# A hybrid encoder trunk: the gate's low-rank path formed from its own mixed input, and the first head group's gating placed in the stream beside the second group's recurrence

## The chip, the cores and the metric

The kernel runs on one core of one Trainium2 chip. A core has five instruction streams that run side by side: PE (TensorE, matrix multiplication), DVE (VectorE), ACT (ScalarE), POOL (GpSimd) and SP (SyncE, which only issues transfers here). Each stream executes in its own order. PE has a second row in the profile, PEld, for its weight loads. The metric is the device time of one execution in microseconds (us); lower is better. The time before is the median of three runs.

## What is computed

Two residual layers over 512 tokens of width 1024, each a token mixer and a gated convolution feed-forward part. The change touches the second layer's mixer alone, an RWKV-7 time mixing with 16 heads of 64:

```python
xx = token_shift(h) - h
xr = h + xx * mu[0]                     # likewise xw, xk, xv, xa, xg
r = xr @ w_r;  k = xk @ w_k;  v = xv @ w_v
w = -softplus(-(w0 + tanh(xw @ w1) @ w2)) - 0.5     # low rank, 64
a = sigmoid(a0 + (xa @ a1) @ a2)                    # low rank, 64
g = sigmoid(xg @ g1) @ g2                           # low rank, 160
...
y = wkv7_scan(r_h, decay, k_h, v_h, -kk, kk * a_h)  # 512 steps in time
...
return (y * g) @ w_o
```

`h` is the RMS-normed residual stream. The gate `g` is needed only when the recurrence has its result `y`.

## The kernel before

Activations lie transposed: 8 tiles of 128 channels by 512 tokens. Every matrix product with weights is done in three matmuls per tile (`mm3`, L284 to L286): high part by high part, high by low, low by high, each 128x128 by 128x512. `split` (L212 on ACT, L213 on DVE or POOL) makes the parts. `weights` loads 128x1024 of a weight matrix into a ring of two tiles `w` (called `w32` in the code) and splits it into a ring of four tiles `wh` and `wl`.

The layer runs in these stages:

- The feed-forward part of layer 0 (`ffn`). Beside it `make_parts` splits the matrices `wk` and `wv` ahead and stores the parts in memory, so that later loads need no split.
- `rwkv_first`: the low-rank first factors for w and a (`l1`), then those for g (`g1a`, `g1b`), then `r`. The low-rank products are taken from the operand `hx` that is not yet divided by the norm and not yet shifted, once with weights scaled by `1 - mu` and once by `mu`; `shifted` then multiplies both results by the norm `rb` and adds the second one shifted by a token. For w and a that is 2 products of 24 matmuls. For g it is 48 matmuls for 128 of the 160 columns and 24 for the other 32 twice. The three tiles of `sigmoid(xg @ g1)`, called `sg`, are stored to memory (`sgd`). After that each tile of `h` is normalized in place, `mix` forms `xr` from it (one ACT operation, one DVE operation, then the split), and `r` takes 12 matmuls for each of the 8 tiles of its first half (`wra`) and as many for the second half (`wrb`).
- `pairs`, for the 8 pairs of heads, woven with `projections` (`k` and `v`).
- `scan(0)`, then `scan(1)`: the recurrence in chunks of 64 tokens, 8 chunks for each group of 4 pairs of heads; I number the 16 chunks c0 to c15. A chunk is a chain: PE L1066, DVE copy L1068 (`wt`), PE L1079, copies L1080 on DVE and L1081 on ACT (`vu`), PE L1086, DVE L1089, and then L1066 of the next chunk. `load` brings each chunk's operands by SP. `invert(1)` is woven into scan(0); it prepares matrices that scan(1) needs. `finish` normalizes the result of two chunks, and after every second call it gates it (L1133, L1135, L1138, L1139), with weights that `gate_weights` has loaded and split at chunk 1 of each scan.
- `project` multiplies by `w_o`: 12 matmuls for each of 8 output tiles and each group, 192 in all. Group 0's half may start when group 0 is gated. It adds to `h`, which `back` reloads from memory (`hd`) since the tile in the chip holds the normalized `h`.

`weave` sets the order around the change. It takes steps of a main generator (the scan), and after each step it takes steps of a `fill` generator (the rest of `projections` in scan(0), `project` in scan(1)), `rate` of them on average. A scheduler then fixes each engine's order from that, from the free tiles of each ring and from the marks that `issue_after` sets. In the profile's lines the rings' names are `w`, `wh`, `wl`; `mxh` and `mxl` are the parts of an activation tile.

Of the kernel before, what the change touches and what calls it, by code (L numbers as in the profile page):

```python
# [19 lines left out]
P = 128  # L20
# [10 lines left out]
RATES = ((1.9, 2), (1.9, 6, 2.2), (0.8, 2, 2), (0.7, 2), (2, 2), (0.7, 6, 2.2))  # L31
LEAD = 6
# [43 lines left out]
def layout(inp):  # L76
# [34 lines left out]
    a["g1a"] = g1[:, :, :P].reshape(P, 1024)  # L111
    a["g1b"] = np.concatenate([g1[:, :, P:], g1[:, :, P:]], axis=2).reshape(P, 512)
# [31 lines left out]
class Emit:  # L144
    def __init__(self, ctx, tc, A, out):
# [24 lines left out]
        self.wd = {n: [dp.tile([P, 2, 1024], F32, name=f"{n}d{m}") for m in range(KT)] for n in PARTS}  # L170
        self.n = self.turn = 0
# [69 lines left out]
    def make_parts(self, pool):  # L241

        nc = self.nc
        at = [(n, m, slice(c, c + 512)) for n in PARTS for m in range(KT) for c in (0, 512)]
        w = []
        for i in range(len(at) + 1):
            with self.tc.issue_after(self.last(mybir.EngineType.Activation)):
                if i < len(at):
                    n, m, c = at[i]
                    w.append(pool.tile([P, 512], F32, tag="pw", bufs=2, name=self.uid("pw")))  # L250
                    nc.sync.dma_start(w[i], self.A[n][m][:, c])
                if i:
                    n, m, c = at[i - 1]
                    for j, x in enumerate(self.split(pool, w[i - 1], [P, 512], "pw", bufs=1)):
                        nc.sync.dma_start(self.wd[n][m][:, j, c], x.bitcast(F32))
            yield

    def parts(self, n, m, whole):
# [13 lines left out]
        return 512, t  # L272

# [310 lines left out]
    def rwkv(self, gain):  # L584
        nc, tc, A = self.nc, self.tc, self.A
        V, S, G = nc.vector, nc.scalar, nc.gpsimd
        with ExitStack() as ctx:
# [7 lines left out]
            r.sgd = dp.tile([3, P, T], F32, name="sgd")  # L595
# [12 lines left out]
            def mix(i, k):  # L608
# [5 lines left out]
                return self.operand(t, lo_eng=(G, V)[k % 2])  # L614
# [6 lines left out]
    def rwkv_first(self, r, ep):  # L621
# [5 lines left out]
        r.sg = [ep.tile([P, T], F32R, name=f"sg{i}") for i in range(3)]  # L627

# [3 lines left out]
        def lowrank(n, w):  # L632
            a = self.acc()
            self.dense(a[0:n], w, hx, ncol=n)
            return a[0:n]
# [9 lines left out]
        def shifted(now, before, n):  # L645
            t, u = tmp("lt", 2), tmp("lu", 2, T + 1)
            G.memset(u[:, 0:1], 0.0)
            V.tensor_tensor(t[0:n], now, rb[0:n], ALU.mult)
            V.tensor_tensor(u[0:n, 1:], before, rb[0:n], ALU.mult)
            G.tensor_tensor(t[0:n], t[0:n], u[0:n, 0:T], ALU.add)  # L650
            return t
# [3 lines left out]
        t = shifted(*lw, P)  # L655
        S.activation(t[0:64], t[0:64], AF.Tanh)

        for j, x in enumerate(r.lr):
            hi, lo = slice(64 * j, 64 * j + 64), slice(64 - 64 * j, 128 - 64 * j)
            S.copy(x[hi], t[hi])  # L660
            V.tensor_tensor(x[lo], t[hi], x[hi].bitcast(F32), ALU.subtract)
# [4 lines left out]
        for kk in range(4):  # L666
            w = self.weights(A["wra"][kk])
            for j in range(2):
# [4 lines left out]
                for m in range(4):  # L673
                    self.mm3(accs[m], self.wcols(w, j * 512 + m * P, P), xs[k], k == 0, k == KT - 1)
        for m in range(4):
            S.copy(r.rt[0][:, m, :], accs[m])


        for i, (x, n) in enumerate(((ga, P), ((gb[0:32], gb[32:64]), 32))):
            t = shifted(*x, n)[0:n]  # L680
            S.activation(t, t, AF.Tanh, scale=0.5)
            V.tensor_scalar(t, t, 0.5, 0.5, ALU.mult, ALU.add)
            if i == 0:
                S.copy(r.sg[0], t)
                V.tensor_tensor(r.sg[1], t, r.sg[0].bitcast(F32), ALU.subtract)
            else:
                self.stack(r.sg[2], t)
        for i, n in enumerate((P, P, 96)):
            nc.sync.dma_start(r.sgd[i, 0:n], r.sg[i][0:n].bitcast(F32))
# [13 lines left out]
    def rwkv_main(self, r, ctx, gain):  # L703
# [38 lines left out]
        def projections():  # L742

            load = Ahead([lambda n=n, m=m: self.parts(n, m, m % 3 == 2) for n in PARTS for m in range(KT)])
# [258 lines left out]

        def gate_weights(g):
            if not sg:
                for i, n in enumerate((P, P, 96)):
                    sg.append(ep.tile([P, T], F32R, name=f"sg{i}"))
                    nc.sync.dma_start(sg[i][0:n].bitcast(F32), r.sgd[i, 0:n])
# [9 lines left out]
        chunks, outs, gated = {}, {}, set()  # L1018

        def load(g, c):  # L1020
            ps = slice(4 * g, 4 * g + 4)
# [12 lines left out]
        left, sg = [], []  # L1034
# [67 lines left out]
        def finish(g, b, y):  # L1102
# [18 lines left out]
            if b % 2 == 1:  # L1121
                hs = slice((b - 1) * P, (b + 1) * P)
                yield
                if b == 1:
# [158 lines left out]
```

## Time and profile before

| what | us |
|---|---|
| median of three runs | 1319.26 (1318.08 to 1319.82) |
| the profiled execution, its own time | 1317.32 |
| its span, first to last instruction | 1315.5 |
| mean granted TensorE clock | 0.978 of full speed |
| PE busy | 1272.7 |
| DVE busy | 848.5 |
| ACT busy | 623.8 |

A line of a timeline gives the start and the length in us, the engine, the line of the kernel, the operation, the tile written and the tiles read, their shapes and how often, and in brackets how long the engine sat idle before it and what it waited for. An engine's name with a q (ACTq, SPq) marks the issue of a transfer. A line of the stretch view gives the stretch, its length, and then for PE, PEld, DVE, ACT and POOL the busy us in it with the number of instructions started, then the granted clock, the share of the DMA engines and GB/s. PE's matmuls are pipelined: a line says 0.39 us for one of 128x512, while the next one starts 0.23 us after it.

### The profile page before, as it was taken

Reading aid. Unit: us, or ns where it says so; the run is one execution under the profiler, and the core shown is the slowest. Engines: PE = TensorE matmul, PEld = TensorE weight load, DVE = VectorE, ACT = ScalarE, POOL = GpSimd, SP = SyncE. Lnnn points to the kernel's source line nnn. Section 1 sums busy time; section 2 is a strip of 40 time slices with the busy share of each in tenths; the row PEclk is TensorE's granted clock in tenths of the full one; section 3 lists DMA queues with packets and bytes.
Section 4 is the critical chain, followed back from the end, with each engine's and each line's share of the span. In section 5 each row is a group of like instructions: output and inputs, shape, how many; then the busy total and the mean of one; then the engine's idle time right before and its main releaser. Section 6 shows DMA issues by size and latency. Waiting matters only on the chain.

```text
span 1315.5 us, 19526 instructions
## 1 busy us (share of the span) xinstructions
PE 1272.7 (97%) x7618; PEld 1031.3 (78%) x7618; DVE 848.5 (64%) x1365; ACT 623.8 (47%) x1062; POOL 142.8 (11%) x152
## 2 busy tenths in 40 slices
PE   8999999999999999999999998898999999999996
PEld 6878888888888888787777766676888888888886
DVE  5565488788874444865869785656687777772223
ACT  5444455555554333565657644333554444442221
POOL 3100200000000010310111012332300000000001
PEclk9999999999999999999979996999999999999998
DMA  7332345555556753245877786881333232333322
GB/s 259 88 113 80 106 151 170 167 168 174 166 173 211 224 150 108 79 136 157 251 220 205 225 209 147 207 221 41 96 96 97 96 96 96 97 92 91 101 89 76
DMA packets 100461, 188.55 MB, mean 143 GB/s; under 512 B 16912, under 2 KB 47760, under 8 KB 100368
## 3 DMA queue, kind: packets, MB, share of 16 engines
q10 hardware_dynamic: 36448, 109.46, 27.2%
q1 hardware_dynamic: 63920, 77.84, 20.7%
q8 instruction: 60, 0.98, 0.3%
q14 instruction: 33, 0.27, 0.1%
HBM read 146.70 MB, written 40.57 MB: 142 GB/s over the span
## 4 chain that ended last, share of the span: by engine, by line
PE 78%; DVE 9%; ACT 3%; issue 2%; DMA 2%; POOL 1%; ACTq 0%; DVEq 0%; SPq 0%; POOLq 0%
PE mm L284 8%; PE mm L285 8%; PE mm L286 8%; PE e L284 5%; PE e L286 5%; PE e L285 5%; PE us L284 5%; PE us L286 5%; PE us L285 5%; PE aux L284 5%; PE aux L286 5%; PE aux L285 5%; DVE tt L971 1%; DVE pr L970 1%; PE us L1066 1%
## 5 line engine op out<-in xcount | busy, mean ns | idle before, releaser
L212 ACT CAST wh<-w 128x512 fp32r<-128x512 f32 (+1 forms) x361 | 220.1, 612 | 398.8 <-PE mm L285 97.1
L213 DVE TENSOR_TENSOR wl<-w,wh 128x512 fp32r<-128x512 f32 x353 | 243.8, 692 | 186.9 <-ACT wh L212 182.8
L284 PE MATMUL mm<-mxh,wh 128*128 128x512 f32 x392 | 161.2, 412 | 0.6 <-DVE h L1166 0.4
L285 PE MATMUL mm<-mxl,wh 128*128 128x512 f32 x392 | 155.7, 397 | 0.6 <-DVE mxl L1139 0.6
L286 PE MATMUL mm<-mxh,wl 128*128 128x512 f32 x392 | 155.9, 398 | 0.3 <-DVE wl L213 0.3
L311 POOL TENSOR_TENSOR ss<-ss,sq 128x512 f32<-128x512 f32 x30 | 40.7, 1357 | 777.3 <-issue 594.8
L284 PEld LDWEIGHTS mm<-mxh,wh 128*128 128x128 f32 x392 | 74.8, 191 | 20.1 <-issue 3.2
L507 ACT ACTIVATE cv<-z,par 128x512 f32<-128x512 f32 x88 | 71.7, 817 | 36.0 <-DVE z L505 35.9
L286 PEld LDWEIGHTS mm<-mxh,wl 128*128 128x128 f32 x392 | 74.7, 191 | 17.3 <-DVE wl L213 0.6
L285 PEld LDWEIGHTS mm<-mxl,wh 128*128 128x128 f32 x392 | 74.8, 191 | 16.3 <-DVE mxl L1139 1.3
L284 PE MATMUL e<-mxh,wh 128*128 128x512 f32 x216 | 84.5, 391 | 0.0
L284 PE MATMUL us<-mxh,wh 128*128 128x512 f32 (+1 forms) x216 | 84.4, 391 | 0.0
L286 PE MATMUL us<-mxh,wl 128*128 128x512 f32 (+1 forms) x216 | 84.1, 389 | 0.0
L285 PE MATMUL us<-mxl,wh 128*128 128x512 f32 (+1 forms) x216 | 84.1, 389 | 0.0
L285 PE MATMUL e<-mxl,wh 128*128 128x512 f32 x216 | 84.0, 389 | 0.0
L286 PE MATMUL e<-mxh,wl 128*128 128x512 f32 x216 | 84.0, 389 | 0.0
L508 DVE SCALAR_TENSOR_TENSOR cv<-z,par,cv 128x512 f32<-128x512 f32 x88 | 66.1, 752 | 23.9 <-ACT cv L507 23.9
L284 PE MATMUL aux<-mxh,wh 128*128 128x512 f32 x208 | 81.2, 391 | 0.2 <-ACT wh L212 0.2
L286 PE MATMUL aux<-mxh,wl 128*128 128x512 f32 x208 | 81.1, 390 | 0.0
L285 PE MATMUL aux<-mxl,wh 128*128 128x512 f32 x208 | 80.9, 389 | 0.0
L509 DVE SCALAR_TENSOR_TENSOR cv<-z,par,cv 128x512 f32<-128x512 f32 x88 | 66.0, 752 | 2.9
L284 PEld LDWEIGHTS e<-mxh,wh 128*128 128x128 f32 x216 | 40.6, 188 | 8.7 <-issue 0.5
(1071 smaller groups left out, 2679.4 us busy)
## 6 DMA issues: line engine op xcount, KB each, us to landing
w<-in_wup ACTq DMA_DIRECT2D x88, 512.0 KB, 3.5
w<-in_wdn ACTq DMA_DIRECT2D x32, 512.0 KB, 3.6
st<-std SPq DMA_DIRECT2D x32, 384.0 KB, 5.8
std<-lq SPq DMA_DIRECT2D x32, 256.0 KB, 4.6
w<-in_wdn ACTq DMA_DIRECT2D x16, 384.0 KB, 3.3
w<-in_wsu ACTq DMA_DIRECT2D x8, 512.0 KB, 3.5
w<-in_wso ACTq DMA_DIRECT2D x8, 512.0 KB, 3.5
pw<-in_wk SPq DMA_DIRECT2D x16, 256.0 KB, 3.9
```

What stands on the lines that cost most here:

```text
L212: nc.scalar.copy(hi[r, :n], src)
L213: (lo_eng or nc.vector).tensor_tensor(lo[r, :n], src, hi[r, :n].bitcast(F32), ALU.subtract)
L284: mm(acc, wh, xh, start=first, stop=False)
L285: mm(acc, wh, xl, start=False, stop=False)
L286: mm(acc, wl, xh, start=False, stop=last)
L311: nc.gpsimd.tensor_tensor(self.ss, self.ss, self.sq, ALU.add)
L507: nc.scalar.activation(c, z[:, 2:], AF.Identity, scale=cw(2, i), bias=self.p("conv_b", l * 44 + i))
L508: nc.vector.scalar_tensor_tensor(c, z[:, 1:T + 1], cw(1, i), c, ALU.mult, ALU.add)
L509: nc.vector.scalar_tensor_tensor(c, z[:, 0:T], cw(0, i), c, ALU.mult, ALU.add)
L970: V.tensor_tensor(q, a, b, ALU.mult)
L971: V.tensor_tensor(tt[:, 0:nj, j + 1:32], tt[:, 0:nj, j + 1:32], q, ALU.add)
L1066: nc.tensor.matmul(us[H[hd], 0, i, :], ar(i, hd, 0), vu[:, hd, i, :], start=True, stop=True)
```

## The change

- `xg` is now formed as `xr`, `xk` and `xv` are, from the normalized `h`, and multiplied by `g1` directly: 24 matmuls for 128 columns and 24 for 32, instead of 72. This stands in a new generator, `gates`, that runs as fill at the start of scan(1), ahead of `project`.
- `g1` is split ahead by `make_parts` (three more steps beside the feed-forward part) and loaded as parts by `gate_parts`.
- `gates` also holds the load of `g2` for group 0, the sigmoid, group 0's gating over all 512 tokens at once (4 tiles of 4 matmuls 128x512), and then the load of `g2` for group 1. `finish` gates group 1 alone, as before in halves of 256 tokens.
- The tiles `sg` stay in the chip; the store and the reload (`sgd`) go. The reload of `h` waits until `gates` has read the normalized tile.
- In `rwkv_first` the low-rank products for w and a are cut into pieces so that the norm's matmuls stand between them, and `lowrank` (scaling, shift, tanh) comes after the second pair of tiles of `wra`.
- Of the low parts of a mixed tile, the even tiles' now go to DVE and the odd ones' to POOL; before it was the other way.
- Table entries: `RATES[2]` (scan(0)) from (0.8, 2, 2) to (0.65, 2, 1), `RATES[3]` (scan(1)) from (0.7, 2) to (0.9, 2), and `LEAD` (fill steps ahead of scan(0)) from 6 to 3.

```diff
-RATES = ((1.9, 2), (1.9, 6, 2.2), (0.8, 2, 2), (0.7, 2), (2, 2), (0.7, 6, 2.2))
-LEAD = 6
+RATES = ((1.9, 2), (1.9, 6, 2.2), (0.65, 2, 1), (0.9, 2), (2, 2), (0.7, 6, 2.2))
+LEAD = 3
...
-                return self.operand(t, lo_eng=(G, V)[k % 2])
+                return self.operand(t, lo_eng=(V, G)[k % 2])
...
-        lw = [lowrank(P, self.first)]
+        lw = [self.acc() for _ in range(2)]
+        self.dense(lw[0], self.first, hx[:4], last=False)
         norm = self.rstd()
         next(norm)
-        lw.append(lowrank(P, w))
+        self.dense(lw[0], self.first, hx[4:], first=False, c0=4 * P)
+        self.dense(lw[1], w, hx[:2], last=False)
         rb = next(norm)
+        self.dense(lw[1], w, hx[2:], first=False, c0=2 * P)
...
-        ga = [lowrank(P, self.lowrank_weights(A["g1a"], P, [f[:, :, 5]])) for f in (om, mu)]
-        gb = lowrank(64, self.lowrank_weights(A["g1b"], 64, [om[:, :, 5], mu[:, :, 5]]))
...
+        def gates():
+            gw[0] = gate_weights(0)
+            ws = self.gate_parts()
+            yield
+            accs = [self.acc("mm")[0:n] for n in (P, 32)]
+            for k in range(KT):
+                with ExitStack() as behind:
+                    for eng in (mybir.EngineType.DVE, mybir.EngineType.Activation):
+                        behind.enter_context(tc.issue_after(self.last(eng)))
+                    j, t = 5 * KT + k, scratch("sq")
+                    S.activation(t, self.hz[k][:, 0:T], AF.Copy, scale=self.p("mu", j))
+                    V.scalar_tensor_tensor(t, self.h[k], self.omu[:, j:j + 1], t, ALU.mult, ALU.add)
+                    x = self.operand(t)
+                for a, w, n in zip(accs, ws, (P, 32)):
+                    self.mm3(a, self.wcols(w, k * n, n), x, k == 0, k == KT - 1)
+                yield
...
+            while 0 not in normed:
+                yield
+            for i in range(4):
+                gate(0, i, slice(0, T))
+                yield
+            gated.add(0)
+            gw[1] = gate_weights(1)
...
-                if c == 1:
-                    with ExitStack() as behind:
-                        for eng in (mybir.EngineType.DVE, mybir.EngineType.Activation):
-                            behind.enter_context(tc.issue_after(self.last(eng)))
-                        gw[g] = gate_weights(g)
...
-        fill = project()
+        fill = itertools.chain(gates(), project())
```

Three places show how the order moves. The first is DVE's stream after the norm's sum in `rwkv_first`. Before, with the gate's weights `w` (L371 scales them, L213 forms their low parts) and the two scalings `lt` and `lu` ahead of the first normalized tiles `h` (L671):

```order
L336 TENSOR_SCALAR rs_4425<-e_4415 128x4
L213 TENSOR_TENSOR wl_4468<-w_861_4460,wh_4467 128x512
L371 TENSOR_TENSOR w_873_4532<-w_873_4532,omu 128x8x32
L371 TENSOR_TENSOR w_873_4532<-w_873_4532,par 128x8x32
L648 TENSOR_TENSOR lt_4565<-aux_4390,rb_4458 128x512
L649 TENSOR_TENSOR lu_4566<-us_4428,rb_4458 128x512
L671 SCALAR_TENSOR_TENSOR h_66<-h_66,par,rb_4458 128x512
L671 SCALAR_TENSOR_TENSOR h_67<-h_67,par,rb_4458 128x512
```

And now, with the mixed tile `mt` (L623) right behind:

```order
L347 TENSOR_SCALAR rs_4435<-us_4425 128x4
L214 TENSOR_TENSOR wl_4488<-w_874_4485,wh_4487 128x512
L672 SCALAR_TENSOR_TENSOR h_66<-h_66,par,rb_4461 128x512
L672 SCALAR_TENSOR_TENSOR h_67<-h_67,par,rb_4461 128x512
L214 TENSOR_TENSOR wl_4540<-w_885_4537,wh_4539 128x512
L623 SCALAR_TENSOR_TENSOR mt_4497<-h_66,omu,mt_4497 128x512
L623 SCALAR_TENSOR_TENSOR mt_4518<-h_67,omu,mt_4518 128x512
L672 SCALAR_TENSOR_TENSOR h_68<-h_68,par,rb_4461 128x512
L214 TENSOR_TENSOR mxl_4501<-mt_4497,mxh_4500 128x512
```

The gate's weights are gone from it, and the low-rank scaling has moved behind the first mixed tiles.

The second place is ACT's stream around chunk c0 in scan(0), where `gwh` and `gw` are the split gate weights that wait for the transfer `w<-in_g` of `g2`. Before, behind the first chunk's copy `vu` (L1081):

```order
L1081 COPY vu_6773<-us_6882 64x256
L780 COPY v_6965<-mm_6829 128x512
L1011 DMA w_1351_6988<-in_g 128x512
L1094 COPY y_6881<-e_6883 64x4x64 x2
L1012 DMA w_1351_6988<-in_g 32x512
L212 CAST gwh_6995<-w_1351_6988 128x512
```

And now, ahead of it (L1120 is the same copy), together with the loads of `g1`'s parts:

```order
L1052 DMA w_1431_7633<-in_g 128x512
L774 COPY v_6772<-mm_6643 128x512
L1053 DMA w_1431_7633<-in_g 32x512
L281 DMA w_1435_7644<-g1d 128x1024
L213 CAST gwh_7640<-w_1431_7633 128x512
L225 CAST gw_7636<-w_1431_7633 32x512
L281 DMA w_1436_7645<-g1d 128x1024
L1120 COPY vu_6668<-us_6731 64x256
```

So the wait for group 0's gate weights has moved from between c0 and c1 to a place before c0's first copy.

The third place is DVE's stream in scan(1), where the parts of `w_o` (`wl`) and of group 1's gate weights (`gw`, `gwl`) come up. Before, between the copies `wt` of c9 and c10:

```order
L1068 COPY wt_7841<-us_7831 128x256
L1080 COPY vu_7743<-us_7831 64x256
L1135 TENSOR_TENSOR rt_4362<-rt_4362,aux_7873 128x2x256
L213 TENSOR_TENSOR wl_7906<-w_1470_7903,wh_7905 128x512
L226 TENSOR_TENSOR gw_7823<-w_1459_7820,gw_7823 32x512
L213 TENSOR_TENSOR gwl_7828<-w_1459_7820,gwh_7827 128x512
L1089 TENSOR_TENSOR vu_7814<-us_7831,wt_7851 64x256 x2
L1166 TENSOR_TENSOR h_66<-h_66,mm_7923 128x512
L1068 COPY wt_7975<-us_7965 128x256
```

And now, from the copy `wt` of c13 (L1107) to the last link of that chunk (L1128):

```order
L1107 COPY wt_8110<-us_8100 128x256
L1119 COPY vu_7997<-us_8100 64x256
L214 TENSOR_TENSOR wl_8178<-w_1531_8175,wh_8177 128x512
L1042 TENSOR_TENSOR rt_4386<-rt_4386,aux_8152 128x512
L227 TENSOR_TENSOR gw_8165<-w_1527_8162,gw_8165 32x512
L214 TENSOR_TENSOR gwl_8170<-w_1527_8162,gwh_8169 128x512
L1196 TENSOR_TENSOR h_66<-h_66,mm_8195 128x512
L1042 TENSOR_TENSOR rt_4387<-rt_4387,aux_8202 128x256
L1128 TENSOR_TENSOR vu_8094<-us_8100,wt_8120 64x256 x2
```

The two loads meet the recurrence four chunks later, and the first sum of `project` (`h_66`, L1196) now stands ahead of the chunk's last link.

More of the change, by code (lines that the diff above doesn't have):

```diff
@@ new lines, in gate @@
+        def gate(g, i, ts):
+            wh, wl, ws = gw[g]
+            c, n = slice(i * P, (i + 1) * P), ts.stop - ts.start
+            q = self.acc("aux")[:, 0:n]
+            self.mm3(q, (wh[:, c], wl[:, c]), [x[:, ts] for x in r.sg[0:2]], True, False)
+            nc.tensor.matmul(q, ws[0:96, c], r.sg[2][0:96, ts], start=False, stop=True)
+            o = rt[g][:, i, ts]
+            V.tensor_tensor(o, o, q, ALU.mult)
+            while len(outs[g]) <= i:
+                outs[g].append(tuple(self.xr.tile([P, T], F32R, tag=t, bufs=10, name=self.uid(t)) for t in ("mxh", "mxl")))
+            oh, ol = (x[:, ts] for x in outs[g][i])
+            S.copy(oh, o)
+            V.tensor_tensor(ol, o, oh.bitcast(F32), ALU.subtract)
@@ L1015, in gate_weights @@
             return (*self.split(ep, w32[:, 0:512], [P, 512], "gw", bufs=1), ws)
[L1018 removed]
+        chunks, outs, gated, normed = {}, ([], []), set(), set()
         def load(g, c):
+            while 4 * g + 3 not in vdone:
+                next(fill)
             ps = slice(4 * g, 4 * g + 4)
@@ L1192, in rwkv_main @@
             pass
-        while 3 not in vdone:
-            next(fill)
         ctx.close()
@@ L1198, in rwkv_main @@
         gw = {}
+        r.sg = [ep.tile([P, T], F32R, name=f"sg{i}") for i in range(3)]
         load(0, 0)
```

113 lines of the change are left out of this document (52 added, 61 removed).

## The prediction

> **What bounds the kernel now.** I began with the totals of the page and the chain that ended last: they say which engine a saving has to reach.
>
> ```profile
> span 1315.5 us, 19526 instructions
> PE 1272.7 (97%) x7618; PEld 1031.3 (78%) x7618; DVE 848.5 (64%) x1365; ACT 623.8 (47%) x1062; POOL 142.8 (11%) x152
> PE 78%; DVE 9%; ACT 3%; issue 2%; DMA 2%; POOL 1%; ACTq 0%; DVEq 0%; SPq 0%; POOLq 0%
> ```
>
> PE is busy in 1272.7 of 1315.5 us and holds 78% of the chain. 42.8 us of idle PE are left. So a matmul that goes saves its time only where PE is full, and a matmul that comes costs nothing only where PE is idle. The second view is therefore the table of stretches, cut at the stages that the change touches.
>
> ```profile
> 400.00:500.00 100.00, 100.00 (x431) 80.41 (x430) 42.50 (x63) 34.79 (x61) 6.88 (x5) 1.00 0.60 186
> 532.89:549.41 16.52, 16.52 (x75) 12.32 (x74) 16.03 (x22) 8.65 (x15) 3.48 (x3) 1.00 0.30 96
> 549.41:571.17 21.76, 21.76 (x97) 18.02 (x96) 20.61 (x27) 16.52 (x29) 9.54 (x7) 1.00 0.34 107
> 597.00:758.00 161.00, 155.48 (x1332) 119.05 (x1332) 120.62 (x217) 104.44 (x195) 22.53 (x21) 0.95 0.74 214
> 758.00:774.20 16.20, 15.48 (x96) 11.29 (x95) 12.52 (x31) 8.47 (x17) 1.97 (x5) 1.00 0.89 213
> 774.20:840.00 65.80, 54.81 (x951) 45.17 (x952) 42.35 (x99) 28.48 (x59) 14.93 (x19) 0.82 0.75 176
> 840.00:897.60 57.60, 53.98 (x690) 41.09 (x687) 35.93 (x78) 20.37 (x47) 20.25 (x21) 0.94 0.74 188
> 897.60:941.00 43.40, 39.32 (x201) 31.93 (x201) 28.81 (x46) 19.22 (x35) 15.21 (x15) 0.96 0.22 68
> ```
>
> In order these are: the feed-forward part of layer 0, where `make_parts` runs; the gate's 72 low-rank matmuls; the 96 matmuls of `wra`; `pairs`; the approach to the recurrence; scan(0), from c0's copy `wt` to c8's; scan(1), up to c15's; and the tail up to the sums of the next norm. Two things matter. In the gate's stretch PE has no idle time, but DVE is also busy for 16.03 of 16.52 us, so what PE loses there DVE may give back as waiting. In scan(0) PE idles 65.80 − 54.81 = 11.0 us, in scan(1) 3.6, in the tail 4.1: that is the room for 48 new matmuls.
>
> All sums are made against the profiled execution: 1317.32 us, 1.8 more than its span. The median of the runs is 1319.26, that is 1.9 above it, and I add 1.9 at the end.
>
> **Part A, the first stage.** The 72 matmuls go: −16.5 us, their stretch (0.229 each; `wra`'s 96 take 21.76, 0.227 each). What is late next is the mixed input of `wra`. These rows price it.
>
> ```profile
> 533.17 0.59 ACT L329 COPY rb<-mm 128x512 f32<-128x512 f32 x1 [0.50 <-PE mm L326]
> 545.09 0.74 DVE L671 SCALAR_TENSOR_TENSOR h<-h,par,rb 128x512 f32<-128x512 f32 x1
> 554.42 0.72 ACT L612 ACTIVATE mt<-h,par 128x512 f32<-128x512 f32 x1
> 559.69 0.74 DVE L613 SCALAR_TENSOR_TENSOR mt<-h,omu,mt 128x512 f32<-128x512 f32 x1
> 556.89 0.62 ACT L212 CAST mxh<-mt 128x512 fp32r<-128x512 f32 x1 [0.68 <-DVE mt L613]
> 545.76 0.68 DVE L213 TENSOR_TENSOR mxl<-mt,mxh 128x512 fp32r<-128x512 f32 x1
> 549.82 1.30 POOL L213 TENSOR_TENSOR mxl<-mt,mxh 128x512 fp32r<-128x512 f32 x1 [5.80 <-ACT mxh L212]
> ```
>
> The norm `rb` was ready at 533.17 + 0.59 = 533.8, behind both low-rank products. In the new order 18 matmuls of the second product follow it, so it comes 18 x 0.227 = 4.1 us earlier, near 529.7, while the second product still ends near 533.0. The first input then needs h 0.74, ACT 0.72, DVE 0.74 and the cast 0.62, 2.8 us in all: 532.5, just in time. Each later input feeds 12 matmuls, 2.72 us of PE. On DVE the eight inputs cost 8 x (0.74 + 0.74), four low parts of 0.68 and some ten weight parts of 0.68, 21.4 us, against PE's 21.8: nearly a tie, so PE will wait at some inputs. Following the new order by hand through these durations I get waits of 0.4, 0.9, 0.85 and 0.6 us at four inputs, and 0.5 for the POOL low parts: 3.3. **A = −16.5 + 3.3 = −13.2.** The bounds are −16.5 (no wait) and, if DVE sets the pace throughout, only what leaves DVE there. I take the hand-followed value, nearer the first, because DVE also starts 4.1 us earlier.
>
> The three new steps of `make_parts` lie beside the feed-forward part, whose row above shows PE busy for 100.00 of 100.00 us with DVE at 42.5 and ACT at 34.8: nothing, and without that cover three loads with a cast (0.62) and a difference (0.68) each, under 4 us. `pairs` is changed only by three `sg` tiles that stay in the chip and a reload that leaves its time; I put 0 (±1).
>
> **Part B, up to c0 and scan(0).** The rows are c0's operand load on SP, copies `wt` of c0, c1 and c2, the wait for the gate's weights, and two gating matmuls.
>
> ```profile
> 763.62 0.50 SPq L1026 DMA_DIRECT2D st<-std  x1
> 774.24 0.42 DVE L1068 COPY wt<-us 128x256 f32<-128x256 f32 x1
> 782.23 0.62 ACT L212 CAST gwh<-w 128x512 fp32r<-128x512 f32 x1 [3.02 <-DMA w<-in_g]
> 785.64 0.42 DVE L1068 COPY wt<-us 128x256 f32<-128x256 f32 x1
> 792.72 0.42 DVE L1068 COPY wt<-us 128x256 f32<-128x256 f32 x1
> 825.59 0.28 PE L284 MATMUL aux<-sg,gwh 128*128 128x256 f32 x1
> 825.71 0.29 PE L285 MATMUL aux<-sg,gwh 128*128 128x256 f32 x1
> 900.00:910.00 10.00, 6.93 (x51) 5.45 (x46) 5.72 (x11) 2.97 (x6) 2.86 (x2) 0.94 0.23 74
> 910.00:920.00 10.00, 9.35 (x42) 7.83 (x42) 5.76 (x12) 4.29 (x9) 0.82 (x5) 0.89 0.08 30
> 660.00:670.00 10.00, 10.00 (x51) 8.20 (x50) 5.47 (x10) 5.98 (x12) 0.39 (x2) 0.51 0.71 204
> ```
>
> c0's first copy follows the issue of its load by 774.24 − 763.62 = 10.6 us. The new loads of `g2` and of `g1`'s parts (some 1.3 MB) and the wait of ACT for them now fall into that time. Queued behind the waiting cast are the copy of `v` and c0's `vu`, but c0 waits for its own load anyway: 0, or the 3.02 us of that row if the cover is gone. LEAD = 3 takes about 14 matmuls from before c0, so PE idles there by about 5 us and the matmuls come back behind it.
>
> From c0 to c1 it took 11.40 us, with that 3.02 us wait and its followers in it; from c1 to c2, 7.08. With the wait gone I put 7.1: −4.3. The first half's gating, 16 matmuls 0.12 apart, leaves: −1.9. The 14 matmuls come in: 14 x 0.227 = +3.2. The moved end of the inversion adds some +0.6, my estimate. That makes −2.4. A gap of 3.1 us in the stretch from 900 is followed by a stretch at clock 0.89; from this I charge +1.1 for the gap before c0, ten us at 0.89. **B = −1.3**, between −4.3 (PE's idle 11.0 us takes all that comes in) and +3.0 (the load wait in the open).
>
> A rule speaks against this step. The Trainium skill, page "TensorE: Matmul & The Clock Gate", section "Part 1: The HAM clock gate", has the clock fall to half rate after an idle window of about 3.4 us and come back after as long a busy one. By that rule the gap before c0 would cost 3.4 x 0.5 = 1.7 us, an estimate from that page, and B would be −0.7. The row from 900 agrees that a gap goes ahead of a slower clock; the row from 660, clock 0.51 with PE busy for all of its 10.00 us, shows the low clock in a stretch without a gap, so gaps are not the only cause here.
>
> **Part C, scan(1).** The copies `wt` of c9, c10, c13 and c14, and the cast that waited for `w_o`:
>
> ```profile
> 845.45 0.42 DVE L1068 COPY wt<-us 128x256 f32<-128x256 f32 x1
> 849.26 1.14 ACT L212 CAST wh<-w 128x512 fp32r<-128x512 f32 x2 [4.97 <-DMA w<-in_wo]
> 859.07 0.43 DVE L1068 COPY wt<-us 128x256 f32<-128x256 f32 x1
> 881.69 0.42 DVE L1068 COPY wt<-us 128x256 f32<-128x256 f32 x1
> 890.89 0.42 DVE L1068 COPY wt<-us 128x256 f32<-128x256 f32 x1 [0.17 <-PE us L1066]
> ```
>
> From c9 to c10 it took 13.62 us, with ACT and DVE held by the loads of `w_o` and `g2`. That goes, and at the neighbours' 7 us the gain is −6.6. In the new order the same two loads meet c13: ahead of c13's last link on DVE stand `wl`, `gw`, `gwl` and the first sum into `h`. From c13 to c14 it took 881.69 to 890.89, 9.20 us; I put 14.2, a little over the interval that these loads made before: +5.0. Fill: before, 78 matmuls of `project` and 32 half-width gating ones, 17.7 + 3.8 = 21.5 us; now 48 for `xg`, 16 gating ones full and 16 half width, 42 of `project`, 24.0 + 1.9 = 25.9. Of the 4.4 more, PE's idle 3.6 us could take most, but idle time on a chain isn't filled whole; +1.6. The mixing of `xg` is 8 x (0.72 + 0.62 on ACT, 0.74 + 0.68 on DVE) = 22.1 us, marked to come behind what both engines had. DVE is busy for 35.93 of 57.60 us and ACT for 20.37, so I put it beside PE's work at nothing; its other end is all 22.1 on the chain. **C = −6.6 + 5.0 + 1.6 = 0**, between −5.0 and +22.1.
>
> **Part D, the tail.** 36 matmuls of `project` that stood in scan(1) now stand behind c15: +8.2. The tail's idle was 43.40 − 39.32 = 4.1; more matmuls at hand cover 3.6 of it, and at full clock instead of 0.96 the stretch is 1.7 shorter. **D = 8.2 − 3.6 − 1.7 = +2.9**, between +8.2 and 0. The reload of `h` now queues on SP behind the last chunks' loads; nothing is behind it, and it is first needed by the sum of an output tile, after 12 matmuls.
>
> **The sum**: −13.2 − 1.3 + 0 + 2.9 = −11.6. 1317.32 − 11.6 = 1305.7, and 1.9 more for the median: **1307.7 us**.
>
> **The rivals.** R1, the inputs bound the first stage: DVE is packed, and the earlier `rb` brings nothing. Then only the gate's own DVE work is won.
>
> ```profile
> 549.61 0.68 DVE L648 TENSOR_TENSOR lt<-aux,rb 128x512 f32<-128x512 f32 x1
> 550.21 0.68 DVE L649 TENSOR_TENSOR lu<-e,rb 128x512 f32<-128x512 f32 x1
> 556.78 1.77 DVE L685 TENSOR_TENSOR sg<-lt,sg 128x512 fp32r<-128x512 f32 x1
> 564.37 0.68 DVE L226 TENSOR_TENSOR sg<-lt,sg 32x512 fp32r<-32x512 f32 x1
> ```
>
> Six scalings at 0.6 apart, 3.7, the differences 1.8 and 0.7, and two short steps of the sigmoid of about 0.4 each: 7.0. The gain shrinks by 6.2: 1313.9. For it speaks DVE's 16.03 of 16.52 us; against it that part of its work there can now wait behind the inputs. Chance 0.12.
>
> R2, slower than before: the mixing of `xg` lands on the recurrence's chain. Each of its eight inputs is 2.76 us of ACT and DVE in turn, and a chunk's copies `wt` and `vu` stand in the same queues. All of it serial: 1307.7 + 22.1 = 1329.8. It decides from 11.6 / 2.76 = 4.2 inputs: from the fifth on the kernel is slower than before. Against it: DVE idles 21.7 us of scan(1), ACT 37.2. Chance 0.10.
>
> R3, better: the two loads cost nothing at c13, since more matmuls stand by there, and the tail's extra matmuls fill what idles: 1307.7 − 5.0 − 2.9 = 1299.8. For it: PE idles for 7.7 us in scan(1) and the tail. Chance 0.13.
>
> R4, the change doesn't put the new matmuls beside anything: −16.5, and 48 x 0.227 = +10.9 in full, and no other part gains: −5.6, 1313.7. For it: PE is busy for 53.98 of 57.60 us in scan(1). Chance 0.10.
>
> **How the numbers follow.** The forecast has 0.55, its own range 1302 to 1312. The range from 1298 to 1318 takes in R1, R3 and R4 and leaves out R2 and a little beside it. A measurement of this kernel can tell about 0.2%, 2.6 us, from no change. Forecast and R3 are faster, and R1 and R4 too but for 0.06, where B or C come out at their upper ends: faster 0.84, same 0.06, slower 0.10.
>
> **What would show it.** A: the stretch from the end of the low-rank products to the end of `wra`, about 25 us instead of 38.3, with PE's idle time by mixed inputs; 31 speaks for R1. B: c0 to c8 64.5 us, c0 to c1 near 7, clock just after c0. C: c8 to c15 57.6 us, c9 to c10 near 7 and c13 to c14 near 14; with R2 waits for `mt` and `mxh` ahead of `wt`. D: 46.3 us behind c15's copy. Most of all the forecast falls if the recurrence has little idle time that long matmuls can use, or if the transfers that now start ahead of c0 delay its load.

## The result and the profile after

The changed kernel takes 1334.47 us (median, 1330.73 to 1340.64), the kernel before 1318.67 beside it: a ratio of 1.0127, 95% interval 1.0086 to 1.0168. It is slower by 16 us where 11.6 us less were forecast. The profiled execution took 1334.18 us. One execution of the run with useless matmuls below took 3178.73 us and is left out of its median. The page's totals and its chain by engines:

```profile
span 1332.4 us, 19460 instructions
PE 1277.4 (96%) x7578; PEld 1025.6 (77%) x7578; DVE 853.5 (64%) x1371; ACT 630.7 (47%) x1072; POOL 142.1 (11%) x148
PE 76%; DVE 8%; DMA 4%; issue 3%; ACT 3%; POOL 1%; ACTq 0%; SPq 0%; DVEq 0%; POOLq 0%
```

PE has 40 matmuls fewer and yet 4.7 us more busy time: its matmuls ran longer, which points to the clock. The start of the copy `wt` of c0, c8 and c15 cuts both traces at the same places. The second row of the table is another profile of the unchanged kernel.

| kernel | c0 at | c0 to c8 | c8 to c15 | c15 to the end | span |
|---|---|---|---|---|---|
| before | 774.24 | 65.80 | 57.55 | 417.91 | 1315.5 |
| before, second profile | 775.43 | 65.11 | 54.99 | 417.97 | 1313.5 |
| changed | 761.12 | 75.85 | 72.68 | 422.75 | 1332.4 |
| changed less before | −13.1 | +10.1 | +15.1 | +4.8 | +16.9 |

c0 comes 13.1 us earlier, and the two recurrences and the tail lose more than twice that. Stretches of the changed kernel (the 96 matmuls of `wra`, from the start of the first to the end of the last, then the three columns of the table, the last as 45 us):

```profile
533.17:559.68 26.51, 23.48 (x98) 17.67 (x98) 24.13 (x30) 16.77 (x29) 8.31 (x6) 1.00 0.27 80
761.12:836.97 75.85, 65.73 (x959) 51.45 (x961) 39.49 (x93) 27.75 (x58) 14.82 (x19) 0.77 0.66 152
836.97:909.65 72.68, 63.45 (x698) 42.87 (x694) 49.79 (x97) 32.38 (x65) 20.09 (x19) 0.93 0.68 170
909.65:954.65 45.00, 43.22 (x233) 34.61 (x229) 29.86 (x49) 19.98 (x37) 16.96 (x16) 1.00 0.23 71
```

In scan(0) the clock is 0.77 on average (0.82 before) and PE is busy 10.9 us longer; in scan(1) PE is busy 9.5 us longer and idle 9.2 us instead of 3.6. Around c0, from the timeline and from stretches of 2 us:

```profile
756.46 0.30 PE L1105 MATMUL us<-vu,st 128*64 128x64 f32 x2 [3.56 <-DMA w<-in_g]
757.49 0.62 ACT L213 CAST gwh<-w 128x512 fp32r<-128x512 f32 x1 [5.17 <-DMA w<-in_g]
761.12 0.42 DVE L1107 COPY wt<-us 128x256 f32<-128x256 f32 x1
761.60 1.12 PE L1118 MATMUL us<-wt,ti 64*64 64x64 f32 x16 [3.75 <-DVE wt L1107]
754.00:756.00 2.00, 0.00 (x0) 0.00 (x0) 1.83 (x6) 0.00 (x0) 0.00 (x0) 1.00 0.99 208
```

PE stands still for 3.56 us, does c0's first link, and stands still for 3.75 us more. (The first line names `g2`'s load as the one that ended the wait; the second run below tests whether it was that load.) From c0 to c1 it is then at clock 0.56:

```profile
761.12:772.91 11.79, 11.31 (x91) 8.47 (x93) 7.12 (x18) 2.97 (x8) 1.30 (x2) 0.56 1.05 259
772.91:780.71 7.80, 7.80 (x102) 5.54 (x98) 6.55 (x18) 3.04 (x6) 1.25 (x2) 1.00 0.63 153
836.97:848.60 11.63, 7.57 (x92) 4.76 (x88) 5.27 (x9) 3.60 (x8) 3.17 (x3) 0.76 0.97 213
887.51:903.10 15.59, 15.45 (x133) 11.55 (x133) 13.64 (x29) 8.65 (x18) 3.41 (x4) 1.00 0.92 255
```

The third line is c8 to c9, 5.41 us before and 11.63 now; the fourth is c13 to c14. What PE waits for behind c8's copy, from the timeline (`sq` holds the mixed `xg` here):

```profile
839.93 0.88 DVE L1128 TENSOR_TENSOR vu<-us,wt 64x256 f32<-64x256 f32 x2 [0.49 <-PE us L1125]
842.28 1.11 DVE L1011 SCALAR_TENSOR_TENSOR sq<-h,omu,sq 128x512 f32<-128x512 f32 x1
843.42 0.62 ACT L213 CAST mxh<-sq 128x512 fp32r<-128x512 f32 x1 [1.57 <-DVE sq L1011]
844.09 0.80 PE L295 MATMUL mm<-mxh,w 128*128 128x512 f32 x1 [3.24 <-ACT mxh L213]
845.24 0.70 PE L1105 MATMUL us<-vu,st 128*64 128x64 f32 x8
848.60 0.43 DVE L1107 COPY wt<-us 128x256 f32<-128x256 f32 x1 [3.84 <-PE us L1105]
```

c8's last link on DVE (L1128) is done at 840.8, and c9's first link on PE (L1105) has begun by then; its next eight matmuls run only from 845.24. The gate's matmul stands ahead of them in PE's stream, so the chain waits for the first mixed input, and the matmul then takes 0.80 us instead of the usual 0.39.

### The profile page after: what moved, and what is told of

The parts are those of the page before. It is cut to its first block, busy times and chain, and to the rows that moved or that the text cites. A ratio compares the mean times of both kernels' runs of the same rounds, so it can differ in the third digit from the quotient of the medians.

```text
span 1332.4 us, 19460 instructions
## 1 busy us (share of the span) xinstructions
PE 1277.4 (96%) x7578; PEld 1025.6 (77%) x7578; DVE 853.5 (64%) x1371; ACT 630.7 (47%) x1072; POOL 142.1 (11%) x148
## 4 chain that ended last, share of the span: by engine, by line
PE 76%; DVE 8%; DMA 4%; issue 3%; ACT 3%; POOL 1%; ACTq 0%; SPq 0%; DVEq 0%; POOLq 0%
PE mm L295 8%; PE mm L296 7%; PE mm L297 7%; PE aux L296 5%; PE aux L295 5%; PE aux L297 5%; PE us L295 5%; PE us L297 5%; PE us L296 5%; PE e L297 5%; PE e L296 5%; PE e L295 5%; DVE tt L965 1%; DVE pr L964 1%; PE e L1130 1%
## 5 line engine op out<-in xcount | busy, mean ns | idle before, releaser
L213 ACT CAST wh<-w 128x512 fp32r<-128x512 f32 x356 | 217.0, 612 | 386.4 <-PE mm L296 105.7
L295 PE MATMUL mm<-mxh,wh 128*128 128x512 f32 (+1 forms) x384 | 157.4, 410 | 1.6 <-DVE h L1196 1.2
L297 PE MATMUL mm<-mxh,wl 128*128 128x512 f32 (+1 forms) x384 | 153.1, 399 | 0.4 <-DVE wl L214 0.3
L296 PE MATMUL mm<-mxl,wh 128*128 128x512 f32 (+1 forms) x384 | 152.2, 396 | 0.0
L295 PEld LDWEIGHTS mm<-mxh,wh 128*128 128x128 f32 (+1 forms) x384 | 72.2, 188 | 20.6 <-issue 3.6
L297 PEld LDWEIGHTS mm<-mxh,wl 128*128 128x128 f32 (+1 forms) x384 | 72.3, 189 | 18.2 <-issue 0.9
L296 PEld LDWEIGHTS mm<-mxl,wh 128*128 128x128 f32 (+1 forms) x384 | 72.6, 189 | 14.9 <-issue 0.7
L295 PE MATMUL us<-mxh,wh 128*128 128x512 f32 x208 | 81.3, 391 | 0.0
L297 PE MATMUL us<-mxh,wl 128*128 128x512 f32 x208 | 81.0, 389 | 0.0
L296 PE MATMUL us<-mxl,wh 128*128 128x512 f32 x208 | 80.9, 389 | 0.0
```

The source lines that it names most:

```text
L213: nc.scalar.copy(hi[r, :n], src)
L295: mm(acc, wh, xh, start=first, stop=False)
L296: mm(acc, wh, xl, start=False, stop=False)
L297: mm(acc, wl, xh, start=False, stop=last)
```

## The experiments

Each run is compared with the kernel before on the same chip (medians 1317.5 to 1318.0). Stage times in the text are cut as in the table above.

**The fill ahead of c0.**

```diff
-LEAD = 3
+LEAD = 6
```

> The changed kernel with LEAD back at 6, nothing else. Theory A (PE's gaps in the recurrence, and the low granted clock behind each, are what was lost; the gap ahead of c0 was made by LEAD = 3): the 7.3 us of PE idle before c0's first link fall to under 3, the stretch behind c0 runs at clock 1.00 instead of 0.56, and c0 to c8 falls from 75.9 us to about 69. Rival B (the split of the gate's weights ahead of c0's copy wt makes that gap, LEAD does not matter): the gap stays at 6 to 8 us and the time within 2 us of the changed kernel's 1334.5.

Measured: 1323.66 us, ratio 1.0045 (1.0026 to 1.0065), 10.8 us less than the changed kernel. The 20 us ahead of c0's copy, in the changed kernel:

```profile
741.12:761.12 20.00, 12.81 (x128) 10.13 (x120) 15.54 (x33) 9.97 (x19) 3.87 (x6) 0.92 0.88 220
```

and with LEAD = 6, with its c0 to c8:

```profile
741.26:761.26 20.00, 17.84 (x177) 14.01 (x170) 15.44 (x34) 12.03 (x25) 3.87 (x6) 1.00 0.87 209
761.26:826.92 65.66, 51.78 (x936) 41.93 (x938) 39.61 (x94) 26.18 (x54) 14.83 (x19) 0.84 0.78 180
```

c0 comes at the same time in both, 761.1 and 761.3, though PE does 5.0 us more ahead of it: that work was free there. c0 to c8 falls from 75.85 to 65.66. (75.85 is the longest of three profiles with one order of scan(0): two runs below, with xg mixed once and with inputs ahead, took 72.16 and 69.41 there. So the profiles put the fall at 4 to 10 us.) The clock from c0 to c1 is 0.84, not the expected 1.00, but theory A holds and rival B falls.

**The gate's loads held back**, so that nothing of them stands ahead of c0:

```diff
-            gw[0] = gate_weights(0)
-            ws = self.gate_parts()
+            with ExitStack() as behind:
+                for eng in (mybir.EngineType.DVE, mybir.EngineType.Activation):
+                    behind.enter_context(tc.issue_after(self.last(eng)))
+                gw[0] = gate_weights(0)
+                ws = self.gate_parts()
```

> The changed kernel with a mark on the loads of g2 and g1 that holds them behind what DVE and ACT had when gates began (the end of scan(0)). Rival B (the gate's loads and their split ahead of c0 are the loss there): c0's copy wt follows its first link at once, about 3.3 us earlier, clock behind c0 near 1.00, c0 to c8 about 8 us shorter; c8 to c9 up to 4 us longer, as g1's parts now arrive late. Theory A with LEAD as the cause: c0 to c8 shorter by the 3.3 us at most, the slow clock stays.

Measured: 1334.95 us, ratio 1.0120 (1.0096 to 1.0144), no gain over the changed kernel. The wait for `wt` shrank from 3.75 to 1.26 us, but PE's wait ahead of c0's first link stayed, and one of c0's own operands is now named for it:

```profile
763.26 0.30 PE L1108 MATMUL us<-vu,st 128*64 128x64 f32 x2 [4.18 <-DMA vu<-vtd]
```

The low clock stayed too, 0.60 from c0 to c1. c0 to c8 took 68.94 us in this profile, further below 75.85 than theory A allowed, but it can't be told from the 69.41 of a run that holds nothing back. The loads are not the main loss there.

**A busy PE in that gap.** To the kernel just described, useless matmuls ahead of c0:

```diff
         for _ in range(LEAD):
             next(fill, None)
+        with tc.issue_after(self.last(mybir.EngineType.PE)):
+            q = self.acc("aux")
+            for _ in range(7):
+                nc.tensor.matmul(q, self.c("center", P), self.h[0], start=True, stop=True)
```

> The kernel with the mark on the gate's loads (e2_mark), and seven matmuls of a constant by a tile of h, whose result is not used, between the last fill and c0's first link, so that PE is busy while it waits for c0's operands; six real matmuls move behind that link for it. If the low clock behind c0 comes from PE's gap of 4.2 us (clock 0.60 from c0 to c1 in e2_mark): the clock from c0 to c1 is over 0.9, and c0 to c1 takes 7 to 8 us instead of 10.4, although 1.4 us of matmuls are added to it. If the low clock has another cause: clock about 0.6, c0 to c1 11 to 12 us.

Measured: 1324.00 us, ratio 1.0066 (1.0044 to 1.0088). c0 to c1 with the gap:

```profile
765.96:776.38 10.42, 9.95 (x88) 7.80 (x90) 7.12 (x18) 2.97 (x8) 1.30 (x2) 0.60 1.09 219
```

and with the useless matmuls in it:

```profile
760.73:767.93 7.20, 6.73 (x91) 5.16 (x93) 6.38 (x16) 2.57 (x7) 1.30 (x2) 1.00 0.86 193
```

Three matmuls more, 3.2 us less. The gap is the cause of the low clock behind c0: adding work that nobody reads makes the chunk faster. (Of the 11 us between the two medians more than this lies ahead of c0: in the profiles c0 comes at 765.96 and 760.73, a spread that the last run takes up.)

**LEAD = 3 in the kernel before** (`LEAD = 6` to `LEAD = 3` in that kernel, nothing else).

> The kernel before the change with LEAD = 3 and nothing else. If LEAD = 3 costs by itself (the matmuls that filled the wait for c0's operands come behind c0, and the clock falls): c0 at the same time as before, c0 to c8 7 to 12 us longer than 65.8, the time 1325 to 1330. If it costs only together with the gate's loads ahead of c0: within 3 us of before.

Measured: 1324.62 us, ratio 1.0060 (1.0037 to 1.0083), 6.8 us over the kernel before and just under what was expected. c0 to c8 took 70.23 instead of 65.80, 4.4 us more where 7 to 12 were expected; c0 came 2.4 us later, and c8 to c15 took 1.7 us more. The clock from c0 to c1 was 0.63 with none of the gate's loads ahead of c0. The lower LEAD costs by itself, though not all of the 10.8 us that it costs the changed kernel. Over all profiles, the clock from c0 to c1 was 0.56 to 0.66 in the five with LEAD = 3 and no useless matmuls, and 0.72 to 1.00 in the eleven with LEAD = 6.

**xg mixed once**, the other seven inputs left out (`if k == 0:` around the mixing).

> The changed kernel, but xg is mixed once, for channel tile 0, and that operand is used for all eight inputs of the gate's products: the mixing and splitting of seven inputs is left out, the 48 matmuls stay. Theory C (PE, in order, waits for mixed inputs in front of the chunks' links, and loses its clock there): c8 to c15 falls from 72.7 us to about 63. Rival D (the 48 matmuls and the loads of w_o and g2 are the loss in scan(1)): within 3 us of 72.7.

Measured: 1329.78 us, ratio 1.0082 (1.0053 to 1.0111); c8 to c15 65.31 instead of 72.68, where theory C had about 63. Of the 15.1 us lost in scan(1), 7.4 hang on the mixing of the last seven inputs; the wait for the first is still there (c8 to c9 11.63).

**Inputs one step ahead.**

```diff
+            xs = [mixed(0)]
             for k in range(KT):
...
-                    x = self.operand(t)
+                if k + 1 < KT:
+                    xs.append(mixed(k + 1))
                 for a, w, n in zip(accs, ws, (P, 32)):
-                    self.mm3(a, self.wcols(w, k * n, n), x, k == 0, k == KT - 1)
+                    self.mm3(a, self.wcols(w, k * n, n), xs[k], k == 0, k == KT - 1)
```

> The changed kernel, but each input of xg is mixed one step ahead of its matmuls. Theory C: only the first input's wait of 3.2 us is left, c8 to c15 falls by 4 to 8 us, the time to about 1328. Rival (the mixing costs DVE and ACT time on the chunk's chain wherever it stands): within 2 us of the changed kernel.

Measured: 1327.78 us, ratio 1.0082 (1.0053 to 1.0112); c8 to c15 66.48, as theory C had it. All the mixing is done, in nearly the time that it took without: this part of the loss was the order, not the work of DVE and ACT.

**Both repairs together** (LEAD = 6 and inputs ahead).

> The changed kernel with LEAD back at 6 and each input of xg mixed one step ahead. If the two losses are separate (the gap ahead of c0; PE's waits for mixed inputs in scan(1)), their gains add: 10.2 us in c0 to c8 and 6.2 in c8 to c15, about 1317, the time of before. If both runs won the same slow-clock time, under 3 us come on top of LEAD = 6 alone (1323.7).

Measured: 1323.99 us, ratio 1.0050 (1.0034 to 1.0066). By stage the gains do add: c0 to c8 65.28, c8 to c15 66.17. But the median is not below that of LEAD = 6 alone. The stretch from the end of `wrb` to c0, where the order of PE and DVE is the same in both, took 186.1 us here and 178.9 there, at clocks of 0.92 and 0.96. Why the median shows none of the gain in scan(1) isn't settled.

**The first two inputs free** to be mixed early (no mark on them), on top of both repairs.

> LEAD = 6, inputs of xg mixed one step ahead (e5_lead6_ahead), and the first two inputs without the mark that holds them behind scan(0), so that they are ready before scan(1) starts. Theory C: PE's wait of 3.2 us at c8 goes and the clock behind it stays at 1.00, c8 to c9 falls from 11.6 to about 6.5, c8 to c15 to about 61, the time to about 1319. Rival: the next wait takes its place, c8 to c15 stays over 64.

Measured: 1323.66 us, ratio 1.0060 (1.0040 to 1.0081). The profiled execution, 1328.88 us, is the longest of its five. Its c8 to c15:

```profile
843.52:904.15 60.63, 57.05 (x699) 39.96 (x695) 46.90 (x93) 29.36 (x59) 20.26 (x19) 1.00 0.76 196
```

and that of the second profile of the unchanged kernel, also at clock 1.00:

```profile
840.54:895.53 54.99, 51.27 (x689) 38.69 (x685) 35.29 (x77) 20.22 (x46) 20.10 (x21) 1.00 0.79 197
```

Here scan(1) is as expected: c8 to c9 6.62, no low clock. The pair of lines prices the added fill alone: PE is busy 5.8 us longer, and idle 3.6 us where it was idle 3.7. The idle time took none of it, in this one pair. The time came back elsewhere: the two inputs floated into `pairs`, and the stretch from the end of `wrb` to c0 took 198.5 us at clock 0.88. Whether they cause that clock wasn't settled.

**The first two inputs beside c4 and c5.**

```diff
+        def inputs():
+            for k in range(2):
+                xs.append(mixed(k))
+                yield
...
+        fill = itertools.chain(fill, inputs())
         self.weave(scan(0), inv, fill, *RATES[2], ktiles=STEPS[2])
```

> LEAD = 6, inputs of xg one step ahead, and the first two inputs mixed as fill of scan(0) once the projections are done (beside c4 and c5). Theory: as with the free inputs, PE's wait of 3.2 us at c8 and the low clock behind it go (c8 to c9 near 6.6, c8 to c15 near 61), and nothing is added to pairs this time; c0 to c8 stays near 65. With the low-rank stage 12 us shorter and the tail 5 us longer, the sum is 12 less 3 less 5, about 4 us below before: 1314 if pairs take the 179 us of before, up to 1321 if they fall in the slower clocks that other runs showed there (187). Rival: the wait moves on to the next inputs, c8 to c15 stays over 64.

Measured: 1320.01 us, ratio 1.0018 (1.0000 to 1.0035): the best form with the gate beside scan(1), and still not faster than before. c8 to c9 is 6.61, but c9 to c10 is 11.03 at clock 0.85 and c8 to c15 65.58, over 64 as the rival had it. Its mechanism holds only in part. In c9 to c10 PE waits 1.59 us, exactly as with the free inputs, where the clock stayed at 1.00 and the same chunk took 9.58. New is a wait of 3.3 us for the copy `wt` of c14, 1.0 with the free inputs. So the 60.63 above took a full clock that this profile did not get.

**A higher fill rate in scan(1)** on top of that, `RATES[3] = (1.3, 2)`.

> As the kernel before it in this list, with RATES[3] = (1.3, 2) instead of (0.9, 2), so that more of project stands in scan(1) and less behind c15. If the 4.9 us longer tail is project's matmuls that only moved, the tail falls to about 419 and c8 to c15 grows by as much: the same time. If project's matmuls find idle PE in scan(1): 2 to 4 us less in all.

Measured: 1329.47 us, ratio 1.0086 (1.0053 to 1.0118). The tail falls by 1.6 us, to 421.34, and c8 to c15 grows by 5.0, to 70.61. Matmuls of `project` do not find idle PE in scan(1); they push the chain back. The median rises by 9.5 us, which neither case had. In the profiles c8 to c15 and the tail together give 3.5 of it; the rest isn't explained.

**The gate already in scan(0).** Two runs let `gates` follow the projections as fill there:

```diff
+        fill = itertools.chain(fill, gates(), project())
         self.weave(scan(0), inv, fill, *RATES[2], ktiles=STEPS[2])
...
-        for _ in fill:
-            pass
-        fill = itertools.chain(gates(), project())
```

> LEAD = 6, inputs one step ahead, and gates follows the projections as fill already in scan(0), so that the 48 matmuls of xg stand beside c4 to c8, where no fill was left (PE busy 6.64 of 10.32 us at c5, 7.6 of 11.6 at c8). Theory (fill is worth its time only where PE idles, and also keeps the clock up): c0 to c8 grows by under 6 us over the 65.7 of LEAD = 6, c8 to c15 falls to 56 or less, the time is about 1309. Rival (the mixing sits on the chain of whatever chunk it stands beside): c0 to c8 grows by over 10, the time is no better than 1317.

> As the kernel before it in this list, with RATES[2] as before the change, (0.8, 2, 2): the inversion's steps and the fill come sooner. Theory: the inversion's last links stand beside matmuls again and PE's waits at c5 to c7 (5.3 us together) shrink: 2 to 5 us less than with (0.65, 2, 1). Rival (the order of inversion and fill is worth nothing): within 2 us.

Measured: 1323.96 us, ratio 1.0052 (1.0024 to 1.0080), and 1324.73, ratio 1.0043 (1.0015 to 1.0070). c0 to c8 grew to 75.82 and 73.26, c8 to c15 only fell to 65.83 and 63.49, not to 56. The rival holds, with both sets of rates alike within what can be told.

**xg in the first stage.** Recurrences and tables as before the change, the shorter low-rank stage kept, xg's 48 matmuls woven into the first half of `wrb`:

```diff
                 for j in range(2):
                     self.mm3(accs[j], self.wcols(ws[j], k * P, P), xs[k], k == 0, k == KT - 1)
+                if m == 0:
+                    if k + 1 < KT:
+                        xg.append(r.mix(5, k + 1))
+                    for a, n, c in zip(ga, (P, 32), (k * P, 1024 + k * 32)):
+                        self.mm3(a, [x[:, c:c + n] for x in g1], xg[k], k == 0, k == KT - 1)
```

> Recurrences, gating and tables as before the change; only the first stage is changed: the norm early and the 72 gate matmuls gone, as in the changed kernel, and xg mixed and multiplied (48 matmuls) beside the first half of wrb, sg stored and reloaded as before. Prediction by part A as measured (c0 13.1 us earlier) plus 48 x 0.227 = 10.9 in full and up to 2 of waits for inputs: c0 0 to 2 us earlier than before, the time 1316 to 1318. If the early norm's gain depends on an empty wrb stage, slower than before by 2 us or more.

> The kernel with xg in the first stage (e8_first), with the three stores of sg issued by POOL instead of SP, where they stood ahead of the load of the second factors; PE waited 4.0 us for the parts of wk behind them. If those stores delayed the chain of transfers: the 4.0 us wait goes, about 1316, 2 us below before. If the parts come late for another reason (their tiles come free late): no change from 1320.

Measured: 1320.17 us, ratio 1.0026 (1.0012 to 1.0039), and with the stores on POOL 1318.45, ratio 1.0021 (1.0000 to 1.0041). In the first, PE did not wait from the end of `wra` to 592 us; what was won there went at the parts of `wk`, for which PE then waited 4.0 us. With the stores on POOL 3.5 us of waiting stayed, of which 2.6 is ACT's split of the second factors. No gain that can be told. The expectation took c0's 13.1 us for the first stage's; the end of `wra` moved by 11.5 (below), which the 48 matmuls' 10.9 nearly use up, and the next stage's loads take the rest.

**The unchanged kernel again.**

> The kernel before the change, unchanged, for a second profile. If the spread of the stretch from the end of wrb to c0 (178 to 187 us in kernels with the same order there) is scatter of the granted clock and not the change's doing, this profile may differ there from the 179.5 us of the first one, while c0 to c8, c8 to c15 and the tail stay within 2 us of 65.8, 57.6 and 417.9.

Measured: 1315.33 us. From the end of `wrb` to c0 it took 180.6 us (179.5 in the first profile); the kernels with the change's order there took 178.3 to 187.0. So a share of their spread may belong to the change; the runs do not settle how much. c0 to c8 and the tail stayed within the 2 us; c8 to c15 did not, 54.99 instead of 57.55, at clock 1.00 instead of 0.94.

## Why the prediction was wrong, by its own steps

**Part A had the mechanism right and the size 1.7 us too good.** The 96 matmuls of `wra` ended at 559.68 instead of 571.17: −11.5, not −13.2. They took 26.51 us from first to last, 21.76 before. PE's waits for their inputs, from the waits of the first stage:

```profile
PE aux L296 <- POOL mxl L214: 2.0, 2, 1.2
PE aux L296 <- DVE mxl L214: 0.7, 1, 0.7
PE aux L295 <- ACT mxh L213: 0.3, 1, 0.3
```

They are 3.0 us against 3.3 followed by hand, but the split was another: 2.0 at POOL's low parts, put at 0.5, and 1.0 at the others, put at 2.75. So the agreement in the sum is partly luck. What the sum lacked is that PE was busy for 23.48 us with matmuls that took 21.76 before. The waits slow the matmuls beside them: behind one, the second matmul starts 0.33 us after the first, not 0.23. R1, which took 6.2 us off, fell. That c0 is 13.1 us earlier, close to the forecast's 13.2, is luck too: at the end of `wrb` the lead was 11.9, and the rest came in the stretch up to c0, 178.3 us instead of 179.5, with 24 matmuls fewer in it.

**Part B failed, −1.3 against +10.1, at two terms.** The first is "From c0 to c1 it took 11.40 us, with that 3.02 us wait and its followers in it [...] With the wait gone I put 7.1". The interval held hardly any wait of PE. Its row in the kernel before:

```profile
774.24:785.64 11.40, 10.13 (x106) 7.17 (x106) 8.92 (x22) 4.96 (x12) 1.31 (x2) 1.00 0.77 184
```

PE was busy for 10.13 of it. ACT waited 3.02 us for a transfer, and PE worked on fill meanwhile; so with these matmuls in it no more than PE's 1.27 us of idle time could be won. At the same full clock and with 100 matmuls instead of 106 it took 9.31 us (the run with the higher fill rate). It came down to 7.20 only with 91 matmuls in it and the clock held up by useless ones; the matmuls that leave it come behind it. The second term is the clock, +1.1, read off the stretch from 910 to 920 at 0.89. That stretch left out the start: the clock was already 0.70 from 908 to 910, then 0.50 to 912 and 0.95 to 914, 1.7 us in all. And ahead of c0 there were two gaps, not one. The filler run prices them: 3.2 us in c0 to c1 alone. The rule of the Trainium skill (page "TensorE: Matmul & The Clock Gate", section "Part 1: The HAM clock gate"), by which I had weighed 1.7 us, is borne out in its direction and was nearer; the low clock behind c0 lasted longer than its 3.4 us, some ten us of busy PE. The decision behind it, that fill moved from before c0 to behind it costs only its own length, fell with LEAD = 6: c0 came no earlier without that fill, and 10.8 us came back in the median.

**Part C failed, 0 against +15.1.** "That goes, and at the neighbours' 7 us the gain is −6.6": the same mistake, in c9 to c10. Its row before:

```profile
845.45:859.07 13.62, 11.79 (x105) 9.58 (x107) 7.94 (x19) 5.94 (x14) 2.96 (x4) 0.75 0.93 254
```

PE was busy for 11.79 of 13.62 us, in part at a low clock, and in the changed kernel c9 to c10 takes 12.10. At full clock it is 11.45 in the second profile of before and 9.58 with the first two inputs free: 1.9 us won, not 6.6. The +5.0 for c13 to c14 came near in size (+6.4) by luck, since the reason is another: PE is busy for 15.45 of those 15.59 us, with 133 matmuls instead of 111. The fill, put at +1.6 because idle PE would take most of it, costs 5.8, all of it. And "I put it beside PE's work at nothing", the mixing, is the largest term. Taking 54.99 us and 5.8 of fill as above, the other 11.9 us of 72.68 are PE's idle time, 9.2 against 3.7, and busy time of 63.45 against 57.05 for nearly the same matmuls, the low clock. Six and more of that go with the mixing a step ahead. The whole of it, to 60.63, went in one profile with the first two inputs ready too; with them mixed beside c4 and c5 it was 65.58, so the last five us hang on the clock and one more wait.

**Part D** had the mechanism right and the size wrong, +4.8 against +2.9: of the tail's idle time more matmuls covered 2.3 us (4.1 against 1.8 idle in 45 us), not 3.6.

**R2** was the case that came nearest, at 1329.8: the mixing did land on the recurrence's chain. Its mechanism held in part only. It is not that DVE and ACT were short of time, since with the inputs a step ahead 6.2 of the 7.4 us that hang on the mixing went, with all of it still there; it is that PE, in order, stood before a mixed input with the chain's next link behind it. And it stood in scan(1) alone; LEAD's cost in scan(0) was no rival of mine at all. R3 and R4 fell with parts B to D, but R4's mechanism, new matmuls that find no idle PE, is what scan(1) showed.

## What to carry to other kernels

An interval that is long is not an interval in which the bounding engine waits: look at that engine's busy time in it before a removed wait of another engine is booked as a gain. Idle time of the bounding engine on a dependent chain need not be room for fill; here 5.8 us of added matmuls cost 5.8 us. Fill that stands in a wait for a transfer may be worth more than its length, since a gap of a few us can be paid again in the clock behind it; and an input that is formed in the step that consumes it stops an engine that runs in order, so form it a step ahead.

## What the hardware showed

The low clock outlasts its gap, by a time that varies. In the changed kernel, stretches of 2 us:

```profile
758.00:760.00 2.00, 0.00 (x0) 0.00 (x0) 1.80 (x4) 1.24 (x3) 0.00 (x0) 0.50 1.10 299
762.00:764.00 2.00, 2.00 (x20) 1.88 (x16) 1.88 (x5) 0.37 (x1) 0.00 (x0) 0.50 1.03 306
768.00:770.00 2.00, 2.00 (x6) 1.32 (x4) 1.88 (x4) 0.30 (x1) 0.46 (x1) 0.50 1.03 233
772.00:774.00 2.00, 2.00 (x33) 1.38 (x34) 1.66 (x4) 1.12 (x2) 0.00 (x0) 1.00 0.59 124
```

PE is busy without a break from 761.6 on, and the clock is full again only after some ten us of that. Behind the single gap of 3.07 us in the kernel before, which ended at 908.40, it was back at 0.95 in the stretch from 912. A shorter gap may or may not do it: PE waited 1.66 us for c3's copy in the changed kernel and 1.68 us in the run with inputs a step ahead,

```profile
793.93 0.68 PE L1118 MATMUL us<-wt,ti 64*64 64x64 f32 x16 [1.66 <-DVE wt L1107]
795.69 0.68 PE L1124 MATMUL us<-wt,ti 64*64 64x64 f32 x16 [1.68 <-DVE wt L1113]
```

and from c3 to c4 the clock was 0.59 in the first and 1.00 in the second. What decides it isn't shown. Where the clock falls varies between executions of one kernel: with LEAD = 6 ten of them took 1318.78 us at a mean clock of 0.983 up to 1331.77 at 0.973, about 1.3 us for each thousandth. A single profile's stage is therefore only good to a few us: c0 to c8 took 69.41 to 75.85 with one order of the streams.
